# Inner rows of the first FFN and gated rows of the retention laid out in lanes, x moved by one spacer

## The chip, the cores and the metric

The kernel runs on one core of one Trainium2 chip. The metric is the device time of one execution in microseconds; lower is better. "TensorE", "VectorE" (DVE), "ScalarE" (ACT), "GpSimd" (POOL) and "SyncE" (SP) are the engines of the core. TensorE shows up in the profile twice: PE for the matmuls and PEld for the loads of their weights.

## The reference

One step of a two-layer streaming encoder on 288 frames (256 of a prompt, 32 of a running stream), width 2048, in fp32:

```python
# layer 0: gMLP mixer, then FFN; layer 1: retention mixer, then FFN
h, v = gmlp_mix(x, w_a_in, a_ln_g, a_ln_b, a_ws, a_bs, w_a_out)     # or
h, s = retention_mix(x, pos, states, w_b_in, w_b_out)
x = layer_norm(ALPHA * x + h, ln_mix_g[i], ln_mix_b[i])
x = layer_norm(ALPHA * x + swiglu(x, w_ffn_in[i], w_ffn_out[i]), ln_ffn_g[i], ln_ffn_b[i])

def swiglu(x, w_in, w_out):                  # hidden width 5632
    gate, up = jnp.split(x @ w_in, 2, axis=-1)
    return (jax.nn.silu(gate) * up) @ w_out
# end of retention_mix: o is normalised per head (8 heads of 512)
y = (jax.nn.silu(g) * o) @ w_out
```

The large products are `x @ w_in` and `(...) @ w_out` of the gMLP, of the retention and of the two FFNs. The inner rows are `silu(gate) * up`; the gated rows are `silu(g) * o`.

## The kernel before

**Products.** Every fp32 operand of a large product is split into two fp32r parts, high and low, with `hi = f` rounded and `lo = f - hi` (function `split`, a ScalarE copy at L655 and a VectorE subtraction at L656). A product of a 128x128 weight block with a 128x288 tile of rows is three matmuls that add into one PSUM tile: weight high with rows high (L123), weight high with rows low (L124), weight low with rows high (L125). The rows are the moving operand of 288 columns, one for each frame; each matmul has its own weight load.

**Weights.** They lie in HBM in the order of use, eight blocks to a chunk of 512 KB. `Core.prep` loads a chunk over the SP queue (tile `raw`), and splits it into `whi` and `wlo`. `Core.blk` hands out the next block and keeps three chunks ahead.

**Stages.** In order: `a_in` and `a_out` (gMLP), `f_in0` and `f_out0` (FFN of layer 0, in two halves of the hidden width: `f_in0` half 0, `f_out0` half 0, `f_in0` half 1, `f_out0` half 1), `b_in` and `b_out` (retention, in two groups of four heads: `b_in`, `b_out`, `b_in`, `b_out`), and `f_in1` and `f_out1`, again in two halves. In the profile, PSUM tiles carry these names with an `a` ahead (`af_out` is `f_out0` and `f_out1`, `ab_out` is `b_out`). TensorE's program is written out by hand and keeps its order. Each stage makes 16 or more output tiles of 128 rows, one after the other, over all k-tiles. The first four output tiles of a stage's `f_out` or `b_out` run interleaved with a lag of two k-tiles (`Core.group`), the other twelve one by one (`Core.tiles`). After a LayerNorm the first ten output tiles of the next `in` stage are made from rows that are not yet normalised, with eight more columns (`PostNorm.start`, 296 columns).

**Two layouts of rows.** Rows that come out of a stage and go into an `out` stage lie in plain tiles of 320 words for each k-tile (`moving`), behind four words (LEAD). `halves` reads them four words at a time: the last four of the first 144 columns, the last four of the second 144, then the four before, and so on down; PSUM is written in the same order. `x` lies in one tile of 10308 words, in lanes (`Lanes.view`): lane k has 36 blocks that lie 92 words apart (STEP), each with two cells of four words that lie 12 words apart (SIDE). The lanes of the 16 k-tiles, high and low, are interleaved with each other; where each begins is in the table PLACES, in units of four words.

**Two orders of products.** `Core.step` makes the three matmuls of one k-tile (L123 to L125). `Core.turn` takes four k-tiles at once and makes their twelve matmuls in the order of the table TURN (L134); PLACES and TURN belong together: each matmul begins 4 units before the one ahead of it, modulo 16 units. `Core.tiles` uses `turn` only where the rows are `x` (L196), and `step` for everything else and in the groups of four.

**Around it.** `Head` (retention) reuses the eight rooms of gated rows (tags `oh0` to `oh3` and `ol0` to `ol3`, 1280 words each) for the head's other data before the gated rows of that head are written (`pair`, `blocks`, `o_gate`). `rope` makes the rotary products on VectorE with two scratch tiles. The last stage keeps weights in the space of `x`, from word 60 on (L844). Spacers ("shift...") set where the tiles of each pool begin.

Of the kernel before, what the change touches and what calls it, by code (L numbers as in the profile page):

```python
# [10 lines left out]
F32 = mybir.dt.float32  # L11
# [41 lines left out]
TURN = ((0, 0), (1, 1), (1, 0), (0, 1), (2, 0), (0, 3), (0, 2), (1, 3), (1, 2), (2, 3), (2, 2), (2, 1))  # L53
GAMMA = [1.0 - 2.0 ** (-5 - h) for h in range(HEADS)]


class Core:
# [55 lines left out]
    def step(self, ps, w, k, m, x, first, last):  # L113
        mm = self.nc.tensor.matmul
        hi, lo = self.blk(w, k, m)
        xh, xl = x
        if len(xh.shape) == 4:
            n = 8 * xh.shape[1]
            wide, most = cells(ps[:, :n]), cells(ps[:, n - NT:n])
        else:  # L120
            wide = most = halves(ps)
            xh, xl = halves(xh), halves(xl)
        mm(wide, hi, xh, start=first, stop=False)  # L123
        mm(most, hi, xl, start=False, stop=False)  # L124
        mm(wide, lo, xh, start=False, stop=last)  # L125
        if self.soon:
            self.soon.pop()()

    def turn(self, ps, w, ks, m, x, first, last):
        b = [self.blk(w, k, m) for k in ks]  # L130
        v = [x(k) for k in ks]
        out = cells(ps[:, :NT])
        for i, (kind, j) in enumerate(TURN):
            self.nc.tensor.matmul(out, b[j][kind == 2], v[j][kind == 1], start=first and i == 0, stop=last and i == len(TURN) - 1)  # L134
        if self.soon:
            self.soon.pop()()
# [27 lines left out]
    def group(self, w, koff, ks, ms, x, evac, hook=None, lag=2):  # L164

        nk = len(ks)
        lag = [lag * j for j in range(len(ms))]
        ps = {}
        n = 0
        for s in range(nk + lag[-1]):  # L170
            done = []
            for j, m in enumerate(ms):
                i = s - lag[j]
                if 0 <= i < nk:
                    if i == 0:
                        ps[m] = (self.accum if j < 4 else self.bank)(f"a{w}_{m}_{self.ticks}")
                    self.step(ps[m], w, koff + ks[i], m, x(ks[i]), i == 0, i == nk - 1)
                    n += 1
                    if i == nk - 1:
                        done.append(m)  # L180
                    if n % nk == 0:
                        self.tick()
            if hook is not None:
                hook(s)
            for m in done:
                evac(m, ps[m])

    def tiles(self, w, koff, ks, ms, x, evac, grouped=True, lag=2):

        nk = len(ks)  # L190
        if grouped:
            self.group(w, koff, ks, ms[:4], x, evac, lag=lag)
            ms = ms[4:]
        for m in ms:
            p = self.accum(f"a{w}_{m}_{self.ticks}")
            if x == self.x:  # L196
                for i in range(0, nk, 4):
                    self.turn(p, w, ks[i:i + 4], m, x, i == 0, i == nk - 4)
            else:
                for i, k in enumerate(ks):  # L200
                    self.step(p, w, koff + k, m, x(k), i == 0, i == nk - 1)
            evac(m, p)
            self.tick()


class Lanes:


    def __init__(self, t):
        self.t = t  # L210

    def view(self, low, k, lead=0):
        t = self.t
        dims = [list(t.ap[0]), [STEP, NT // 8 + lead], [SIDE, 2], [1, 4]]
        return bass.AP(tensor=t.tensor, offset=t.offset + 4 * PLACES[low][k] - STEP * lead, ap=dims)

    def front(self, k, i):
        t = self.t
        dims = [list(t.ap[0]), [SIDE, 2], [1, 2]]
        return bass.AP(tensor=t.tensor, offset=t.offset + 4 * PLACES[0][k] - STEP + i, ap=dims)  # L220
# [4 lines left out]
    def led(self, k):  # L225
        return self.view(0, k, 1), self.view(1, k)
# [40 lines left out]
class PostNorm:  # L267
# [359 lines left out]
    def start(self, w, ms, evac):  # L627

        core, nc = self.core, self.nc
        x = self.x.led  # L630
# [38 lines left out]
def gmlp(core, cst, x, y, lnp, ins, v_out, begin, load):  # L669
    tc, nc = core.tc, core.nc  # L670
    xs = core.x
    with ExitStack() as es:
# [126 lines left out]
        core.tiles("a_out", 0, list(range(KT)), list(range(KT)), lambda k: (sh[:, k, :NT], late["sl"][:, k, :NT]),  # L799
# [4 lines left out]
def ffn(core, cst, x, y, lnp, layer, prev, out=None, rows=None):  # L804
    tc, nc = core.tc, core.nc
    xs = core.x
    ln = PostNorm(core, cst, x, y, lnp, 2 * layer + 1, out)
    with tc.tile_pool(name=f"ffn{layer}", bufs=1, reuse_waits="tile") as pool:
        if out is None:
            hh = moving(pool, HH, f"hh{layer}")  # L810
            hl = moving(pool, HH, f"hl{layer}")
        else:
            ln.tables(pool, rows)
            pool.tile([P, 36], F32, name="shift_hid")
            hid = pool.tile([P, HH, 2 * ROW], F32R, name="hid")[:, :, LEAD:]
            hh, hl = hid, moving(pool, HH, "hl1")
        for half in range(2):
            sg = {}

            def evac(m, ps):  # L820
# [4 lines left out]
                else:  # L825
# [4 lines left out]
                    split(nc, hh[:, i, :NT], hl[:, i, :NT], f)  # L830
# [17 lines left out]
            core.tiles(f"f_out{layer}", half * HH, list(range(HH)), list(range(KT - ends)),  # L848
                       lambda k: (hh[:, k, :NT], hl[:, k, :NT]),
                       ln.last if half else ln.part)  # L850
# [5 lines left out]
def retention(core, cst, x, y, lnp, prev, ins, st_p_out, st_s_out):  # L856
    tc, nc = core.tc, core.nc
    xs = core.x
    mm = nc.tensor.matmul
    wide = lambda out, l, r, **kw: mm(turned(out, 4), l, turned(r, 4), **kw)  # L860
    with ExitStack() as es:
        pool = es.enter_context(tc.tile_pool(name="ret", bufs=1, reuse_waits="tile"))
        oh, ol = {}, {}
        for i in range(8):
            pool.tile([P, 4 * ROW], F32, tag=f"o{'hl'[i % 2]}{i // 2}", name=f"r_room{i}")
# [15 lines left out]
        def pair(name, h):  # L881
            t = pool.tile([P, 4 * ROW], F32, tag=f"oh{h % 4}", name=name)
            return t[:, :2 * DV].rearrange("p (t f) -> p t f", t=2)

        def blocks(name, h):
            t = pool.tile([P, 4 * ROW], F32, tag=f"ol{h % 4}", name=name)
            return t[:, :4 * NT].rearrange("p (b i s) -> p b i s", b=9, i=4)

        def rope(dst, a, b, cos, sin, nm):
            t1 = pool.tile([P, NT], F32, tag="rt1", name=f"rt1{nm}", bufs=1)  # L890
            t2 = pool.tile([P, NT], F32, tag="rt2", name=f"rt2{nm}", bufs=1)
            nc.vector.tensor_tensor(t1, a[:, :NT], cos, ALU.mult)
            nc.vector.tensor_tensor(t2, b[:, :NT], sin, ALU.mult)
            nc.vector.tensor_tensor(dst[:, 0, :NT], t1, t2, ALU.subtract)
            nc.vector.tensor_tensor(t1, a[:, :NT], sin, ALU.mult)
            nc.vector.tensor_tensor(t2, b[:, :NT], cos, ALU.mult)
            nc.vector.tensor_tensor(dst[:, 1, :NT], t1, t2, ALU.add)

        class Head:
# [206 lines left out]
            def o_gate(self, what):  # L1106
# [6 lines left out]
                oh[h % 4] = moving(pool, 4, f"r_oh{h}", f"oh{h % 4}")  # L1113
                ol[h % 4] = moving(pool, 4, f"r_ol{h}", f"ol{h % 4}")
                for i in range(4):
                    split(nc, oh[h % 4][:, i, :NT], ol[h % 4][:, i, :NT], self.sg[:, i, :])
# [27 lines left out]
        for grp in range(2):  # L1144
            a, b, c, d = order[4 * grp:4 * grp + 4]
            ms = sum(a + b, []) + c[0] + d[0] + c[1] + d[1]
            if grp == 0:
# [4 lines left out]
                       lambda k: (oh[k // 4][:, k % 4, :NT], ol[k // 4][:, k % 4, :NT]),  # L1152
                       ln.last if grp else ln.part)
# [4 lines left out]
def hybrid_step(ctx, tc, ins, outs):  # L1158
# [5 lines left out]
    cp.tile([P, 4], F32, name="shift")  # L1164
    lnp.tile([P, 32], F32, name="shift_lnp")
    x = Lanes(cp.tile([P, LANES], F32R, name="x"))
    core.x = x.pair
# [119 lines left out]
```

## Time and profile before

| | |
|---|---|
| median of 3 runs | 2765.64 us (2765.02 to 2766.17) |
| the profiled execution | 2765.76 us, of which 2763.9 us from the first to the last instruction |
| TensorE busy | 2758.4 us, 100% of the span, 21614 matmuls |
| VectorE, ScalarE, GpSimd busy | 1717.5 us (62%), 1262.7 us (46%), 144.6 us (5%) |
| mean granted TensorE clock | 0.999 |
| data moved | 515.55 MB, 187 GB/s |

Matmuls are pipelined: one takes about 287 ns from its start to its end, but the next starts about 125 ns after it. What a matmul costs is therefore the distance from start to start, which is read from a stretch of time and the number of matmuls in it: the pieces of the chain of waits have a start, a length and a number; the table of stretches (windows) has the number of matmuls that touch each stretch, which is two more than the number that start in it.

### The profile page before, as it was taken

Reading aid. Unit: us, or ns where it says so; the run is one execution under the profiler, and the core shown is the slowest. Engines: PE = TensorE matmul, PEld = TensorE weight load, DVE = VectorE, ACT = ScalarE, POOL = GpSimd, SP = SyncE. Lnnn points to the kernel's source line nnn. Section 1 sums busy time; section 2 is a strip of 40 time slices with the busy share of each in tenths; the row PEclk is TensorE's granted clock in tenths of the full one; section 3 lists DMA queues with packets and bytes.
Section 4 is the critical chain, followed back from the end, with each engine's and each line's share of the span. In section 5 each row is a group of like instructions: output and inputs, shape, how many; then the busy total and the mean of one; then the engine's idle time right before and its main releaser. Section 6 shows DMA issues by size and latency. Waiting matters only on the chain.

```text
span 2763.9 us, 51981 instructions
## 1 busy us (share of the span) xinstructions
PE 2758.4 (100%) x21614; PEld 2748.0 (99%) x21614; DVE 1717.5 (62%) x2779; ACT 1262.7 (46%) x1747; POOL 144.6 (5%) x245
## 2 busy tenths in 40 slices
PE   9999999999999999999999999999999999999999
PEld 9999999999999999999999999999999999999999
DVE  6688964444444466877865666767854455444466
ACT  5454554433344444644543444545644433444444
POOL 1100000000000000012200121200000000000001
PEclk9999999999999999999999999999999999999999
DMA  8654555555555555567765666765455555555554
GB/s 281 217 191 160 171 177 176 177 170 171 175 175 175 181 169 178 171 218 239 243 195 169 201 218 220 230 200 170 169 176 175 177 172 175 171 173 169 173 170 142
DMA packets 147374, 515.55 MB, mean 187 GB/s; under 512 B 18161, under 2 KB 21377, under 8 KB 147105
## 3 DMA queue, kind: packets, MB, share of 16 engines
q1 hardware_dynamic: 132848, 473.62, 52.0%
q0 software_dynamic: 14288, 38.60, 4.5%
q8 instruction: 169, 2.77, 0.4%
q14 instruction: 69, 0.56, 0.1%
HBM read 486.99 MB, written 25.17 MB: 185 GB/s over the span
## 4 chain that ended last, share of the span: by engine, by line
PE 99%; DVE 1%; DMA 0%; issue 0%; POOL 0%; ACT 0%; POOLq 0%; DVEq 0%; ACTq 0%
PE af_in L134 34%; PE ab_in L134 19%; PE af_out L123 6%; PE af_out L124 6%; PE af_out L125 6%; PE aa_in L134 4%; PE ab_out L123 2%; PE ab_out L124 2%; PE ab_out L125 2%; PE af_in L123 2%; PE af_in L125 2%; PE af_in L124 1%; PE aa_out L123 1%; PE aa_out L124 1%; PE aa_out L125 1%; PE sp L860 1%
## 5 line engine op out<-in xcount | busy, mean ns | idle before, releaser
L656 DVE TENSOR_TENSOR wlo<-raw,whi 128x1024 fp32r<-128x1024 f32 (+1 forms) x884 | 1074.7, 1217 | 805.1 <-ACT whi L655 801.9
L655 ACT CAST whi<-raw 128x1024 fp32r<-128x1024 f32 (+1 forms) x884 | 924.7, 1046 | 1301.5 <-PE af_in L134 319.9
L134 PE MATMUL af_in<-x,whi 128*128 128x288 f32 x4992 | 808.5, 287 | 0.0
L134 PEld LDWEIGHTS af_in<-x,whi 128*128 128x128 f32 x4992 | 705.5, 187 | 0.0
L134 PE MATMUL af_in<-x,wlo 128*128 128x288 f32 x2496 | 516.0, 287 | 0.0
L134 PE MATMUL ab_in<-x,whi 128*128 128x288 f32 x2752 | 443.9, 287 | 0.0
L134 PEld LDWEIGHTS af_in<-x,wlo 128*128 128x128 f32 x2496 | 391.0, 187 | 0.0
L134 PEld LDWEIGHTS ab_in<-x,whi 128*128 128x128 f32 x2752 | 388.3, 187 | 1.3
L124 PE MATMUL af_out<-hl,whi 128*128 128x288 f32 x1320 | 383.2, 290 | 0.0
L134 PE MATMUL ab_in<-x,wlo 128*128 128x288 f32 x1376 | 283.2, 286 | 0.0
L124 PEld LDWEIGHTS af_out<-hl,whi 128*128 128x128 f32 x1320 | 247.8, 188 | 0.0
L134 PEld LDWEIGHTS ab_in<-x,wlo 128*128 128x128 f32 x1376 | 215.0, 187 | 0.0
L123 PE MATMUL af_out<-hh,whi 128*128 128x288 f32 x704 | 205.1, 291 | 0.0
L125 PE MATMUL af_out<-hh,wlo 128*128 128x288 f32 x704 | 202.9, 288 | 0.0
L123 PE MATMUL af_out<-hid,whi 128*128 128x288 f32 x616 | 178.4, 290 | 0.0
L125 PE MATMUL af_out<-hid,wlo 128*128 128x288 f32 x616 | 177.9, 289 | 0.0
L123 PE MATMUL ab_out<-r_oh,whi 128*128 128x288 f32 x512 | 149.0, 291 | 0.0
L124 PE MATMUL ab_out<-r_ol,whi 128*128 128x288 f32 x512 | 148.8, 291 | 0.0
L125 PE MATMUL ab_out<-r_oh,wlo 128*128 128x288 f32 x512 | 147.3, 288 | 0.0
L125 PEld LDWEIGHTS af_out<-hh,wlo 128*128 128x128 f32 x704 | 132.3, 188 | 0.2 <-DVE wlo L656 0.2
L123 PEld LDWEIGHTS af_out<-hh,whi 128*128 128x128 f32 x704 | 131.8, 187 | 0.0
L134 PE MATMUL aa_in<-x,whi 128*128 128x288 f32 x768 | 124.2, 287 | 0.0
(301 smaller groups left out, 3572.9 us busy)
## 6 DMA issues: line engine op xcount, KB each, us to landing
raw<-in_wpack_dram SPq DMA_DIRECT2D x883, 512.0 KB, 3.3
v_room<-tv POOLq DMA_DIRECT2D x32, 144.0 KB, 4.6
of<-o_room POOLq DMA_DIRECT2D x32, 144.0 KB, 5.6
vw<-v_room POOLq DMA_DIRECT2D x8, 512.0 KB, 6.0
out_st_s_dram<-sso POOLq DMA_DIRECT2D x16, 256.0 KB, 2.5
out_st_p_dram<-so POOLq DMA_DIRECT2D x16, 256.0 KB, 5.3
o_room<-to POOLq DMA_DIRECT2D x8, 512.0 KB, 3.8
g_room<-g_tv POOLq DMA_DIRECT2D x16, 144.0 KB, 4.3
```

The costliest lines, as they stand in the source:

```text
L123: mm(wide, hi, xh, start=first, stop=False)
L124: mm(most, hi, xl, start=False, stop=False)
L125: mm(wide, lo, xh, start=False, stop=last)
L134: self.nc.tensor.matmul(out, b[j][kind == 2], v[j][kind == 1], start=first and i == 0, stop=last and i == len(TURN) - 1)
L655: pin(nc.scalar.copy(hi, f))
L656: nc.vector.tensor_tensor(lo, f, hi.bitcast(F32), ALU.subtract)
L860: wide = lambda out, l, r, **kw: mm(turned(out, 4), l, turned(r, 4), **kw)
```

## The change

The inner rows of the first FFN (`f_out0`) are written into one tile `h` in lanes as x has them (92 and 12 words), with places of their own (INNER, 22 k-tiles). The gated rows of the retention (`b_out`) are written into the eight rooms, four lanes to a room, with 36 words from block to block and 12 or 76 words between the two cells (GATED); they are read from the last block to the first, and PSUM is written in the matching order, eight columns at a time from the end. The rooms grow from 1280 to 1344 words. Both are now multiplied by `turn`, four k-tiles at a time; where 22 k-tiles leave two over, the table TAIL has their six products. The groups of four output tiles still go through `step`, but read lanes. `f_out1` and `a_out` keep their plain tiles (class Plain, same reading order as before). `rope` writes its first product into its destination and needs one scratch tile instead of two. The spacer of four words in front of x goes; x and all tiles behind it begin 32 bytes earlier, against weights that stay where they are, and the weights kept in the space of x begin at word 64 instead of 60.

```diff
+TAIL = ((0, 0), (1, 1), (1, 0), (0, 1), (2, 0), (2, 1))
+INNER = ((18, 2566, 1722, 894, ...), (1674, 14, 1682, 2502, ...))
+WORDS = 13504
+GATED = ((8, 3), (12, 3), (0, 19), (4, 3))
+OROOM = 1344
...
-    def turn(self, ps, w, ks, m, x, first, last):
-        b = [self.blk(w, k, m) for k in ks]
-        v = [x(k) for k in ks]
-        out = cells(ps[:, :NT])
-        for i, (kind, j) in enumerate(TURN):
-            self.nc.tensor.matmul(out, b[j][kind == 2], v[j][kind == 1], start=first and i == 0, stop=last and i == len(TURN) - 1)
+    def turn(self, ps, w, koff, ks, m, x, first, last):
+        b = [self.blk(w, koff + k, m) for k in ks]
+        order = TURN if len(ks) == 4 else TAIL
+        for i, (kind, j) in enumerate(order):
+            low = int(kind == 1)
+            self.nc.tensor.matmul(x.out(ps, low), b[j][kind == 2], x.moving(low, ks[j]),
+                                  start=first and i == 0, stop=last and i == len(order) - 1)
...
-            if x == self.x:
+            if x.turns:
                 for i in range(0, nk, 4):
-                    self.turn(p, w, ks[i:i + 4], m, x, i == 0, i == nk - 4)
+                    self.turn(p, w, koff, ks[i:i + 4], m, x, i == 0, i + 4 >= nk)
...
+class Gated:
+    turns = True
...
+    def at(self, low, k):
+        first, side = GATED[(k + 2 * low) % 4]
+        return self.rooms[low][k // 4 % 4], 4 * first, 4 * side
...
+    def moving(self, low, k):
+        t, o, side = self.at(low, k)
+        n = NT // 8
+        return bass.AP(tensor=t.tensor, offset=t.offset + o + 36 * (n - 1), ap=[list(t.ap[0]), [-36, n], [side, 2], [1, 4]])
...
+    def out(self, ps, low):
+        return bass.AP(tensor=ps.tensor, offset=ps.offset + NT - 8, ap=[list(ps.ap[0]), [-8, NT // 8], [4, 2], [1, 4]])
...
-            hh = moving(pool, HH, f"hh{layer}")
-            hl = moving(pool, HH, f"hl{layer}")
+            h = Lanes(pool.tile([P, WORDS], F32R, name=f"h{layer}"), INNER)
...
-                    split(nc, hh[:, i, :NT], hl[:, i, :NT], f)
+                    split(nc, *h.pair(i), f if out is not None else cells(f))
...
-                    o = 60 + i * CB * P
+                    o = 64 + i * CB * P
...
-            t1 = pool.tile([P, NT], F32, tag="rt1", name=f"rt1{nm}", bufs=1)
-            t2 = pool.tile([P, NT], F32, tag="rt2", name=f"rt2{nm}", bufs=1)
...
+            t = pool.tile([P, NT], F32, tag="rt", name=f"rt{nm}", bufs=1)
+            for d, (u, v, op) in enumerate(((cos, sin, ALU.subtract), (sin, cos, ALU.add))):
+                r = dst[:, d, :NT]
+                nc.vector.tensor_tensor(r, a[:, :NT], u, ALU.mult)
+                nc.vector.tensor_tensor(t, b[:, :NT], v, ALU.mult)
+                nc.vector.tensor_tensor(r, r, t, op)
...
-                    split(nc, oh[h % 4][:, i, :NT], ol[h % 4][:, i, :NT], self.sg[:, i, :])
+                    split(nc, *gated.pair(4 * (h % 4) + i), cells(self.sg[:, i, :]))
...
-    cp.tile([P, 4], F32, name="shift")
```

On TensorE, the fifth output tile of `f_out0`, the first after the group of four, begins as follows before (tile names are output, rows, weights; `128x36x2x4` is the order of writing of `halves`):

```order
L123 MATMUL af_out_4_96_7065<-hh_3740,whi_6960 128x36x2x4
L124 MATMUL af_out_4_96_7065<-hl_3741,whi_6960 128x36x2x4
L125 MATMUL af_out_4_96_7065<-hh_3740,wlo_6961 128x36x2x4
L123 MATMUL af_out_4_96_7065<-hh_3740,whi_6960 128x36x2x4
L124 MATMUL af_out_4_96_7065<-hl_3741,whi_6960 128x36x2x4
L125 MATMUL af_out_4_96_7065<-hh_3740,wlo_6961 128x36x2x4
```

The same place with the change (L132 is the matmul in `turn`):

```order
L132 MATMUL af_out_4_96_7063<-h_3739,whi_6958 128x288 x4
L132 MATMUL af_out_4_96_7063<-h_3739,wlo_6959 128x288
L132 MATMUL af_out_4_96_7063<-h_3739,whi_6958 128x288 x4
L132 MATMUL af_out_4_96_7063<-h_3739,wlo_6959 128x288 x3
L132 MATMUL af_out_4_96_7063<-h_3739,whi_6958 128x288 x4
```

The number of matmuls and the blocks of weights are the same; within four k-tiles the three kinds of product are mixed, and the output is written as one run of 288 columns. The same tile ends so, with a last full turn of twelve (the first four rows) and the two k-tiles that are left over:

```order
L132 MATMUL af_out_4_96_7063<-h_3739,whi_7022 128x288 x4
L132 MATMUL af_out_4_96_7063<-h_3739,wlo_7023 128x288
L132 MATMUL af_out_4_96_7063<-h_3739,whi_7022 128x288 x4
L132 MATMUL af_out_4_96_7063<-h_3739,wlo_7023 128x288 x3
L132 MATMUL af_out_4_96_7063<-h_3739,whi_7022 128x288 x4
L132 MATMUL af_out_4_96_7063<-h_3739,wlo_7023 128x288 x2
```

The last two rows are the six products of TAIL. In `b_out` the fifth output tile read like the first fence before, with `r_oh` and `r_ol` (the rooms with the high and the low gated rows) for `hh` and `hl`. With the change it begins so, on TensorE:

```order
L132 MATMUL ab_out_220_16688<-r_oh_14235,whi_16583 128x36x8
L132 MATMUL ab_out_220_16688<-r_ol_14236,whi_16583 128x36x8 x2
L132 MATMUL ab_out_220_16688<-r_oh_14235,whi_16583 128x36x8
L132 MATMUL ab_out_220_16688<-r_oh_14235,wlo_16584 128x36x8
L132 MATMUL ab_out_220_16688<-r_oh_14235,whi_16583 128x36x8 x2
L132 MATMUL ab_out_220_16688<-r_ol_14236,whi_16583 128x36x8 x2
L132 MATMUL ab_out_220_16688<-r_oh_14235,wlo_16584 128x36x8 x3
```

There the output is written as 36 runs of eight columns, where it was written in 72 runs of four.

More of the change, by code (lines that the diff above doesn't have):

```diff
@@ L111, in state, with step @@
         return self.ready[c]
-    def step(self, ps, w, k, m, x, first, last):
+    def step(self, ps, w, koff, k, m, x, first, last):
         mm = self.nc.tensor.matmul
[L115 to L125, printed above, removed]
+        b = self.blk(w, koff + k, m)
+        for i, (j, low) in enumerate(((0, 0), (0, 1), (1, 0))):
+            mm(x.out(ps, low), b[j], x.moving(low, k), start=first and i == 0, stop=last and i == 2)
         if self.soon:
             self.soon.pop()()
-    def turn(self, ps, w, ks, m, x, first, last):
-        b = [self.blk(w, k, m) for k in ks]
-        v = [x(k) for k in ks]
-        out = cells(ps[:, :NT])
-        for i, (kind, j) in enumerate(TURN):
-            self.nc.tensor.matmul(out, b[j][kind == 2], v[j][kind == 1], start=first and i == 0, stop=last and i == len(TURN) - 1)
+    def turn(self, ps, w, koff, ks, m, x, first, last):
[5 more added lines that the diff above has]
+                                  start=first and i == 0, stop=last and i == len(order) - 1)
         if self.soon:
@@ L219, in front, with __init__, out, pair @@
         dims = [list(t.ap[0]), [SIDE, 2], [1, 2]]
[L220 removed]
+        return bass.AP(tensor=t.tensor, offset=t.offset + 4 * self.places[0][k] - STEP + i, ap=dims)
     def pair(self, k):
         return self.view(0, k), self.view(1, k)
[L225 to L226 removed]
+    def out(self, ps, low):
+        return cells(ps[:, :NT])
+class Led:
+    turns = False
+    def __init__(self, lanes):
+        self.lanes = lanes
+    def moving(self, low, k):
+        return self.lanes.view(low, k, 1 - low)
+    def out(self, ps, low):
+        return cells(ps[:, 8 * low:8 + NT])
+class Plain:
+    turns = False
+    def __init__(self, hi, lo):
+        self.tiles = hi, lo
+    def pair(self, k):
+        return tuple(t[:, k, :NT] for t in self.tiles)
+    def moving(self, low, k):
+        return halves(self.tiles[low][:, k, :NT])
+    def out(self, ps, low):
+        return halves(ps)
+class Gated:
+    turns = True
+    def __init__(self, hi, lo):
+        self.rooms = hi, lo
+    def at(self, low, k):
+        first, side = GATED[(k + 2 * low) % 4]
+        return self.rooms[low][k // 4 % 4], 4 * first, 4 * side
+    def view(self, low, k):
+        t, o, side = self.at(low, k)
+        return bass.AP(tensor=t.tensor, offset=t.offset + o, ap=[list(t.ap[0]), [36, NT // 8], [side, 2], [1, 4]])
+    def moving(self, low, k):
+        t, o, side = self.at(low, k)
+        n = NT // 8
+        return bass.AP(tensor=t.tensor, offset=t.offset + o + 36 * (n - 1), ap=[list(t.ap[0]), [-36, n], [side, 2], [1, 4]])
+    def pair(self, k):
+        return self.view(0, k), self.view(1, k)
+    def out(self, ps, low):
+        return bass.AP(tensor=ps.tensor, offset=ps.offset + NT - 8, ap=[list(ps.ap[0]), [-8, NT // 8], [4, 2], [1, 4]])
 def cells(v):
@@ L798, in gmlp @@
         ln = PostNorm(core, cst, x, y, lnp, 0)
-        core.tiles("a_out", 0, list(range(KT)), list(range(KT)), lambda k: (sh[:, k, :NT], late["sl"][:, k, :NT]),
+        core.tiles("a_out", 0, list(range(KT)), list(range(KT)), Plain(sh, late["sl"]),
                    lambda m, ps: ln.last(m, ps, True))
```

50 lines of the change are left out of this document (23 added, 27 removed).

## The prediction

> **What bounds the kernel now.** I read the page's engine shares and chain first, since they say which engine can pay anything back.
>
> ```profile
> PE 2758.4 (100%) x21614; PEld 2748.0 (99%) x21614; DVE 1717.5 (62%) x2779; ACT 1262.7 (46%) x1747; POOL 144.6 (5%) x245
> PEclk9999999999999999999999999999999999999999
> PE 99%; DVE 1%; DMA 0%; issue 0%; POOL 0%; ACT 0%; POOLq 0%; DVEq 0%; ACTq 0%
> L134 PE MATMUL af_in<-x,whi 128*128 128x288 f32 x4992 | 808.5, 287 | 0.0
> L124 PE MATMUL af_out<-hl,whi 128*128 128x288 f32 x1320 | 383.2, 290 | 0.0
> ```
>
> TensorE is the chain: 99% of it, at the full granted clock in all 40 slices, with no idle time before the large groups. Nothing is waited for there, so the time is the number of matmuls times their distance from start to start. The number stays at 21614; only the distance can change. A matmul's own length (287 and 290 ns above) hides it, because matmuls overlap. So I took stretches of one kind of matmul each, from the table of stretches for TensorE (from:to, length, PE busy, number of matmuls that touch the stretch, granted clock, DMA share, GB/s):
>
> ```profile
> 720.00:960.00 240.00, 240.00 (x1922) 1.00 0.53 176
> 575.00:705.00 130.00, 130.00 (x1011) 1.00 0.52 171
> 975.00:1015.00 40.00, 40.00 (x313) 1.00 0.53 178
> 1040.00:1100.00 60.00, 60.00 (x476) 1.00 0.55 180
> 1432.00:1525.00 93.00, 93.00 (x724) 1.00 0.51 171
> 1880.00:1940.00 60.00, 60.00 (x476) 1.00 0.52 173
> 2215.00:2340.00 125.00, 125.00 (x989) 1.00 0.52 173
> 2350.00:2600.00 250.00, 250.00 (x1950) 1.00 0.52 171
> ```
>
> Two matmuls in each count only reach into the stretch, so I divide by the count less two. The turned matmuls on x (first row, f_in0's second half): 240/1920 = 125.0 ns. f_out0's first half, plain rows and step: 130/1009 = 128.8. Its second half: 40/311 = 128.6 at first, 60/474 = 126.6 later. b_out's first group: 93/722 = 128.8; late in its second group 60/474 = 126.6. f_out1, also plain rows: 125/987 = 126.6. And the last row is the odd one: f_in1's second half has the same lanes of x, the same order and the same weights' places as the first row, and runs at 250/1948 = 128.3. The chain of waits gives the same prices over whole runs of turned matmuls (start, length, number):
>
> ```profile
> 368.52 204.05 PE af_in L134 x1632
> 708.68 264.00 PE af_in L134 x2112
> 1429.90 0.13 PE ab_out L123
> 1528.89 31.12 PE ab_in L134 x249
> 2009.11 204.05 PE af_in L134 x1632
> 2346.92 271.04 PE af_in L134 x2112
> ```
>
> 264.00/2112 = 125.00 against 271.04/2112 = 128.33; b_out's first group is (1528.89 - 1429.90)/768 = 128.89. The two halves of f_in0 and f_in1 that precede an f_out are both at 204.05/1632 = 125.03. So plain rows know two rates here, 128.89 and 126.67 (I take that for 126.6), and lanes know 125.0 and 128.33. Each holds for whole stages and turns over at a stage's start or after a stall, such as the one for the centering product in f_out0:
>
> ```profile
> 1015.22 0.14 PE cen L363
> ```
>
> **The change part by part.** (1) Turned tiles. 12 of 16 output tiles: f_out0 has 12 x 22 k-tiles x 3 products x 2 halves = 1584 matmuls, b_out 12 x 16 x 3 x 2 groups = 1152. What they cost now: f_out0's first half, 792 at 128.89. Its second half begins at the change from f_in0 (708.68 + 264.00 = 972.68); the group of four takes 264 x 0.12889 = 34.0 us, to 1006.7; until the centering at 1015.22 there are 66 more at 128.89, and the remaining 726 run at 126.67. b_out's first group has 576 at 128.89. In its second, the group of four and one more tile (48) are at 128.89 if the stall falls where it does in f_out0, one tile after the group's end; the other 528 are at 126.67. Together 1482 at 128.89 and 1254 at 126.67. The price with the change is bounded by the two rates of x in lanes, 125.0 and 128.33. I take 125.0: of 12768 turned matmuls in this trace (rows under rival C) 10656 are at 125.0 and 2112 at 128.33, and the new stages come straight after an x stage at 125.0. Gain 1482 x 3.89 + 1254 x 1.67 = 5.76 + 2.09 = 7.9 us; at 128.33 it would be 0.8 - 2.1 = -1.3.
>
> (2) The groups of four keep step but read lanes: 528 + 384 = 912 matmuls, now at 128.89. Step over lanes is in the trace twice:
>
> ```profile
> 30.00:53.00 23.00, 23.00 (x183) 1.00 0.86 285
> 315.00:365.00 50.00, 50.00 (x386) 1.00 0.51 169
> 1229.83 2.66 PE sp L860 x12
> ```
>
> a_in's first tiles: 23/181 = 127.1. f_in0's first ten tiles: 50/384 = 130.2, but two of three have 296 columns. A 512-column matmul on the same page costs 2.66/12 = 222 ns, so a column costs (222 - 125)/224 = 0.43 ns and the eight columns 3.5; two thirds of that off gives 127.9. I take 127.6: 912 x 1.3 = 1.2 us, between -1.2 (at 130.2) and 1.6.
>
> (3) TAIL: six products end with one jump that breaks the even steps. 24 tiles have it. By (2) such jumps cost 2 to 3 ns on average, so 0.1 us; 1 us if each upset several turns.
>
> (4) ScalarE and VectorE write lanes instead of plain rows: 76 splits. Lanes are priced in the trace by x's own split:
>
> ```profile
> L655 ACT CAST x<-y 128x288 fp32r<-128x288 f32 x64 | 26.8, 429 | 13.1 <-PE af_in L125 5.7 <-DMA y<-in_xT_dram 4.8 <-PE ab_in L125 2.5
> L655 ACT CAST hh<-hf 128x288 fp32r<-128x288 f32 x44 | 18.9, 430 | 2.6 <-DVE hf L829 2.6
> L656 DVE TENSOR_TENSOR x<-y,x 128x288 fp32r<-128x288 f32 x64 | 27.1, 451 | 6.2 <-ACT x L655 6.1
> L656 DVE TENSOR_TENSOR hl<-hf,hh 128x288 fp32r<-128x288 f32 x44 | 19.9, 451 | 0.6 <-ACT hh L655 0.5
> ```
>
> 429 against 430 ns and 451 against 451: nothing. rope keeps six VectorE operations per call, all in VectorE's own order, and VectorE is at 62%; nothing. What covers these is TensorE's 24 matmuls per weight chunk, 3.0 us at 125.0, against one ScalarE half of a weight split and one VectorE half:
>
> ```profile
> L656 DVE TENSOR_TENSOR wlo<-raw,whi 128x1024 fp32r<-128x1024 f32 (+1 forms) x884 | 1074.7, 1217 | 805.1 <-ACT whi L655 801.9
> L655 ACT CAST whi<-raw 128x1024 fp32r<-128x1024 f32 (+1 forms) x884 | 924.7, 1046 | 1301.5 <-PE af_in L134 319.9
> ```
>
> 1.05 and 1.22 us in each 3.0 leave over half of both engines free. With that cover gone, the 76 splits would cost at most 76 x 0.45 = 34 us on either engine. The first matmuls of f_out0 and b_out wait for the same weights as before, with no new wait on the rows.
>
> (5) x and all later tiles move 32 bytes against the weights. The trace has no other place for x. Its price is bounded by the same 125.0 and 128.33 on one side and, where it is now 128.33, by 125.0 on the other. Plain rows give the nearest hint: f_out0's and f_out1's lie in pools with different bases, and both show the same two rates. So I take the place to leave the rates alone: 0, between -35 and +7 us (rivals below).
>
> Sum: 7.9 + 1.2 - 0.1 = 9.0 us. The profiled execution took 2765.76 us, its span 2763.9 and 1.9 around it; 2756.8 is left. The median shown is 2765.64, 0.1 lower, inside the rounding: **2756.8 us**.
>
> **The rivals.** A: moving x also frees f_in1's second half. It is the one lane stage at 128.33, and it enters from f_out1's plain rows, which move too. 2112 x 3.33 = 7.0 us more: 2749.8. For it: the rate is a matter of where a stage locks in. Against: x, f_out1's rows and their distance to each other move together. 17%.
>
> B: the lanes are not what makes 125.0, and the new stages lock in at 128.33. For it: f_in1's second half is exactly that. Against: all other x stages, among them those right behind b_in's small products. Then (1) gives -1.3, and with (2) and (3) the sum is -0.2: 2765.9, no change. 13%. The Trainium skill, "TensorE: Matmul & The Clock Gate", Part 2, gives TensorE two independent SBUF read ports, so that loading weights takes nothing from the moving rows. By it the place of rows would not matter and the sum would be zero; the rows at 125.0, 126.6 and 128.8 for equal shapes disagree.
>
> C: slower. With x 32 bytes lower against the weights, its turned matmuls lock in at 128.33 in the stages that are at 125.0 now: f_in0 3744, b_in 4128, f_in1's first half 1632 and a_in 1152, together 10656:
>
> ```profile
> L134 PE MATMUL af_in<-x,wlo 128*128 128x288 f32 x2496 | 516.0, 287 | 0.0
> L134 PE MATMUL ab_in<-x,whi 128*128 128x288 f32 x2752 | 443.9, 287 | 0.0
> L134 PE MATMUL ab_in<-x,wlo 128*128 128x288 f32 x1376 | 283.2, 286 | 0.0
> L134 PE MATMUL aa_in<-x,whi 128*128 128x288 f32 x768 | 124.2, 287 | 0.0
> L134 PE MATMUL aa_in<-x,wlo 128*128 128x288 f32 x384 | 79.2, 287 | 0.1
> ```
>
> With the 4992 quoted first these are 12768, less the 2112 of f_in1's second half. All of them cost 35.5 us: 2765.7 - 9.0 + 35.5 = 2792. It decides from 4360 matmuls on, (9.0 + 5.5)/0.00333, two half stages and a bit. For it: the same addresses have been at 128.33 once. Against: behind b_in's small products the rate comes back to 125.0 each time, as in the two rows below (6.01/48 and 42.02/336). 12%.
>
> ```profile
> 1223.82 6.01 PE ab_in L134 x48
> 1232.49 42.02 PE ab_in L134 x336
> ```
>
> D: b_out is written to PSUM in runs of eight columns, backwards. Runs of four have never been under 126.6 here, one run of 288 is at 125.0. If runs cost, b_out's 1152 turned matmuls stay at 126.67: 1.9 us less gain, 2758.7. 8%. "PSUM — Partial Sum Buffer", Specifications, in the Trainium skill says that any non-contiguous pattern slows matmuls significantly; the trace bears out at most 1.6 ns in 125.
>
> **How the numbers follow.** Forecast 50%, A 17%, B 13%, C 12%, D 8%. 0.2% is 5.5 us, about what a measurement of this kernel can tell from no change. The forecast, A and D are faster by more than that (75%, of which I leave 2 to their weaker forms, with some stage turning over the wrong way): faster 0.73. B and the mild forms of C, one half stage lost (2763.9), are the same: 0.14. C proper is slower: 0.13. The range runs from A with the better end of (2), 2748, to the sum with two half stages of x lost, 2756.8 + 2 x 7.0 = 2771; I cut it at 2769, since one half stage or B lie well inside. Outside are C proper and A's extremes.
>
> **What would show it.** Right: the stretches of f_out0 and b_out after the group of four at 125.0 (1000 ns hold 8.0 starts), groups at 127 to 128, x stages unchanged. Step (1) falls if af_out or ab_out on the turn's line shows 126.7 or 128.3; (5) falls if a run of turned x matmuls in the chain leaves 125.0, or if f_in1's second half does; (4) if TensorE shows idle time before f_in's or f_out0's groups with a VectorE or ScalarE releaser. A new stage that turns over in the middle would make the sum wrong without making its mechanism wrong.

## The result and the profile after

| | before | after |
|---|---|---|
| median | 2765.33 us of 4 runs (2764.95 to 2766.17) | 2748.72 us of 4 runs (2748.63 to 2750.32) |
| ratio to before | | 0.9941, 95% interval 0.9924 to 0.9958 |
| the profiled execution's span | 2763.9 us | 2746.9 us |

The kernel became faster by 16.6 us, about twice the 9.0 that the sum gave. The page of the changed kernel, its engine shares, its clock and the share of the chain by engine:

```profile
PE 2741.2 (100%) x21614; PEld 2731.1 (99%) x21614; DVE 1714.8 (62%) x2779; ACT 1261.9 (46%) x1747; POOL 144.5 (5%) x245
PEclk9999999999999999999999999999999999999999
PE 99%; DMA 0%; DVE 0%; SPq 0%; ACT 0%; issue 0%; DVEq 0%; ACTq 0%
```

As many matmuls as before, at the same clock, and TensorE is still the whole chain. VectorE and ScalarE are as busy as they were. So nothing but the distance from start to start has changed. The chain of waits of the changed kernel gives it by stage (start, length, number):

```profile
571.03 33.47 PE af_out L123 x264
604.50 99.30 PE af_out L132 x792
703.80 264.02 PE af_in L132 x2112
967.82 33.47 PE af_out L123 x264
1001.29 8.29 PE af_out L132 x66
1009.71 91.07 PE af_out L132 x726
...
1422.44 24.59 PE ab_out L123 x192
1447.03 73.32 PE ab_out L132 x576
1520.35 60.00 PE ab_in L132 x480
...
1870.09 67.22 PE ab_out L132 x528
2000.05 204.01 PE af_in L132 x1632
2204.06 133.76 PE af_out L123 x1056
2337.82 264.00 PE af_in L132 x2112
```

The turned tiles of f_out0 come at 99.30/792 = 125.4 ns, near the 125.0 that was forecast. Those of b_out do not: 73.32/576 = 127.3, a rate that no turned tiles of before have. And the last row is f_in1's second half: 264.00 us where it was 271.04, so 125.0 ns instead of 128.33, on rows whose layout and order the change leaves as they were.

Since each stage begins where the one before it ends, the starts in this view give each stage's length. The difference to before, in us:

| stage | forecast | after | lanes and orders alone | spacer alone |
|---|---|---|---|---|
| f_out0, first half | -3.4 | -3.34 | -2.40 | -2.35 |
| f_out0, second half | -1.8 | -1.90 | -1.12 | -0.74 |
| b_out, first group | -2.5 | -1.07 | -0.37 | -1.71 |
| b_out, second group | -1.3 | +0.09 | +0.80 | -0.54 |
| f_in1, second half | 0 | -7.04 | 0 | -7.04 |
| f_out1, second half | 0 | -0.93 | 0 | -0.93 |
| all else of the span | 0 | -2.8 | -0.4 | -1.8 |
| span | -9.0 | -17.0 | -3.5 | -15.1 |

The forecast column is the prediction's terms laid out by stage: f_out0's first half, for instance, is 792 x 3.89 + 264 x 1.3 ns = 3.4 us. The last two columns are the first two experiments. "All else" holds a_in, whose length differs from run to run (200.7 to 202.3 us over all runs here); the -0.4 of the third column is a_in alone.

### The profile page after: what moved, and what is told of

Its sections match the earlier page's. It is cut to its first block, busy times and chain, and to the rows that moved or that the text cites. A ratio compares the mean times of both kernels' runs of the same rounds, so it can differ in the third digit from the quotient of the medians.

```text
span 2746.9 us, 51972 instructions
## 1 busy us (share of the span) xinstructions
PE 2741.2 (100%) x21614; PEld 2731.1 (99%) x21614; DVE 1714.8 (62%) x2779; ACT 1261.9 (46%) x1747; POOL 144.5 (5%) x245
## 4 chain that ended last, share of the span: by engine, by line
PE 99%; DMA 0%; DVE 0%; SPq 0%; ACT 0%; issue 0%; DVEq 0%; ACTq 0%
PE af_in L132 34%; PE ab_in L132 19%; PE af_out L123 11%; PE af_out L132 7%; PE ab_out L132 5%; PE aa_in L132 5%; PE af_in L123 5%; PE aa_out L123 4%; PE ab_in L123 2%; PE ab_out L123 2%; PE aa_in L123 2%; PE sp L923 1%; PE ob L923 1%; PE b L574 0%; PE p L566 0%; PE q L565 0%
## 5 line engine op out<-in xcount | busy, mean ns | idle before, releaser
L132 PE MATMUL af_in<-x,whi 128*128 128x288 f32 x4992 | 803.5, 286 | 0.0
L132 PEld LDWEIGHTS af_in<-x,whi 128*128 128x128 f32 x4992 | 701.4, 187 | 0.0
L132 PE MATMUL af_in<-x,wlo 128*128 128x288 f32 x2496 | 513.3, 286 | 0.0
L132 PE MATMUL ab_in<-x,whi 128*128 128x288 f32 x2752 | 443.7, 287 | 0.0
L132 PEld LDWEIGHTS af_in<-x,wlo 128*128 128x128 f32 x2496 | 389.4, 187 | 0.0
L132 PEld LDWEIGHTS ab_in<-x,whi 128*128 128x128 f32 x2752 | 387.8, 187 | 1.1
L132 PE MATMUL ab_in<-x,wlo 128*128 128x288 f32 x1376 | 283.0, 286 | 0.0
L132 PEld LDWEIGHTS ab_in<-x,wlo 128*128 128x128 f32 x1376 | 214.7, 187 | 0.0
L123 PE MATMUL af_out<-hl,whi 128*128 128x288 f32 x616 | 177.9, 289 | 0.0
L132 PE MATMUL af_out<-h,whi 128*128 128x288 f32 x1056 | 170.9, 287 | 0.0
L132 PEld LDWEIGHTS af_out<-h,whi 128*128 128x128 f32 x1056 | 148.8, 187 | 0.0
L123 PE MATMUL af_in<-x,whi 128*128 128x296 f32 (+1 forms) x640 | 124.6, 291 | 0.0
L132 PE MATMUL aa_in<-x,whi 128*128 128x288 f32 x768 | 124.3, 287 | 0.0
L123 PEld LDWEIGHTS af_out<-hid,wlo 128*128 128x128 f32 x616 | 115.6, 188 | 0.0
L123 PEld LDWEIGHTS af_out<-hl,whi 128*128 128x128 f32 x616 | 115.6, 188 | 0.0
L123 PEld LDWEIGHTS af_out<-hid,whi 128*128 128x128 f32 x616 | 115.6, 188 | 0.0
L132 PE MATMUL af_out<-h,wlo 128*128 128x288 f32 x528 | 108.8, 287 | 0.0
L132 PEld LDWEIGHTS aa_in<-x,whi 128*128 128x128 f32 x768 | 107.9, 187 | 0.0
```

What stands on the lines that cost most here:

```text
L123: mm(x.out(ps, low), b[j], x.moving(low, k), start=first and i == 0, stop=last and i == 2)
L132: self.nc.tensor.matmul(x.out(ps, low), b[j][kind == 2], x.moving(low, ks[j]), start=first and i == 0, stop=last and i == len(order) - 1)
```

## The experiments

Below, a row's or lane's **place** is where its reading begins (for gated rows that is the last block), counted in units of 16 bytes from the start of the weights' tiles, by the program's addresses. The lanes of one tile all have the same place modulo 4. x is at 2 modulo 4 before and at 0 modulo 4 after; the inner rows' lanes are at 0 modulo 4 and the gated rows' at 1 modulo 4 in the changed kernel, and at 2 and 3 where the spacer is put back into it.

### The two halves of the change, one at a time

The changed kernel with the spacer put back; x and all tiles behind it then lie as in the kernel before:

```diff
-                    o = 64 + i * CB * P
+                    o = 60 + i * CB * P
...
+    cp.tile([P, 4], F32, name="shift")
```

> The changed kernel with the four-word spacer in front of x again (and the kept weights from word 60): all tiles from x on lie 32 bytes higher against the weights, the lanes and the turned order stay. Theory P (the place of the rows against the weights picks which of its rates a stage takes): f_in1's second half goes back from 264.0 to about 271.0 us, f_out1's last stage back to about 141.6, a_out to about 98.9; f_out0 keeps 132.8 and 133.0. Time about 2748.7 + 7.0 + 0.9 + 0.5 + up to 2 for smaller stages = 2757 to 2759. Rival L (the lanes upstream free f_in1's second half by the state in which they leave TensorE): f_in1's second half stays at 264.0, time 2749 to 2751.

Measured: 2762.15 us (10 runs; before 2765.75 on the same chip), ratio 0.9987, interval 0.9978 to 0.9997. That is slower than the 2757 to 2759 that was expected. Its chain of waits, at f_out0's first half, at b_out's first group, and at the end:

```profile
572.15 33.79 PE af_out L123 x264
605.93 99.92 PE af_out L132 x792
...
1425.94 24.70 PE ab_out L123 x192
1450.64 73.92 PE ab_out L132 x576
...
2209.67 133.76 PE af_out L123 x1056
2343.43 271.04 PE af_in L132 x2112
```

With the spacer the turned tiles of f_out0 come at 126.2 ns and those of b_out at 73.92/576 = 128.33, and f_in1's second half is back at 271.04. f_out0's halves were expected to keep 132.8 and 133.0 us and took 133.7 each, so this part of the expectation was wrong. Lanes and orders without the move bring 3.5 us.

The 126.2 is a mean of the two prices that x has. The sixth, seventh and eighth tile of f_out0's first half, one tile of 66 matmuls each and one matmul of the tile ahead:

```profile
613.94 8.38 PE af_out L132 x67
622.20 8.59 PE af_out L132 x67
630.66 8.39 PE af_out L132 x67
```

The seventh is at 8.59/67 = 128.2 ns, its neighbours at 125.1 and 125.2, and so it goes on to the end of the half: every third tile is slow. Each tile ends in the jump of TAIL; x and b_out, whose order has no jump, hold one rate. That the jump turns the rate over is thus likely, but it was not tried at this place.

The other half: the kernel before without its spacer, and nothing else changed.

```diff
-                    o = 60 + i * CB * P
+                    o = 64 + i * CB * P
...
-    cp.tile([P, 4], F32, name="shift")
```

> The kernel before without the spacer and nothing else of the change: all rows 32 bytes lower against the weights, plain rows and step as before. Theory P: f_in1's second half 264.0 us (-7.0), f_out1's last stage 140.7 (-0.9), a_out 98.4 (-0.5), f_in stages -0.3 each; and if plain rows then take 126.67 ns everywhere, f_out0 about 133.8 and 134.0 (-2.3, -0.9) and b_out 97.3 and 97.4 (-1.7, -0.5): 2765.3 - 15 = about 2750. If plain rows keep 128.89 in f_out0 and b_out: 2755 to 2756. Rival L: f_in1's second half stays at 271.0, time 2764 to 2766.

Measured: 2751.01 us (2749.77 to 2751.39, 4 runs), ratio 0.9945, interval 0.9931 to 0.996. The move alone brings 14.7 of the 16.6 us. In its table of stretches (from:to, length, PE busy, matmuls that touch the stretch, clock, DMA share, GB/s) stand f_out0's first half, b_out's first group, and f_in1's second half:

```profile
575.00:700.00 125.00, 125.00 (x989) 1.00 0.53 173
1430.00:1515.00 85.00, 85.00 (x674) 1.00 0.53 174
2345.00:2595.00 250.00, 250.00 (x2002) 1.00 0.53 176
```

Less two for each count: plain rows and step are at 125/987 = 126.6 and 85/672 = 126.5 where the kernel before had 128.8 and 128.8, and x is at 250/2000 = 125.0. So the move took away the plain rows' slow rate and x's slow rate at once, with the old layout and the old order of products. On top of it the lanes and turns bring f_out0 another 1.0 and 1.2 us, and cost b_out 0.6 us in each group (table above, the column after less the column of the spacer alone).

### The place against the weights, or the rows' own place

Without the spacer the rows move and the weights stay. To tell the two apart, the rows were left where they are in the kernel before, and the weights moved 32 bytes the other way:

```diff
-        self.wp.tile([P, 16], F32, tag="shift", name="shift_wp", bufs=1)
+        self.wp.tile([P, 24], F32, tag="shift", name="shift_wp", bufs=1)
...
-                    o = 60 + i * CB * P
+                    o = 64 + i * CB * P
...
-    cp.tile([P, 4], F32, name="shift")
```

(The weights' spacer stands ahead of the weights and of all rows, and grows by 32 bytes; x's spacer, which with its padding takes 32 bytes, goes. So the weights lie 32 bytes further on and the rows where they were.)

> The kernel before, rows at exactly their addresses of before, but the weights' buffers begin 32 bytes higher (their spacer grows from 16 to 24 words, the spacer in front of x goes, and the kept weights follow to word 64). Theory P (the place of the rows against the weights): every stage as in the run with only the spacer gone: f_in1's second half 264.0 us, f_out0 133.8 and 134.1, b_out 97.3 and 97.4; time 2750 to 2752. Rival Q (the rows' own address decides, or the space at the end of memory): stages as before, f_in1's second half 271.0, f_out0 136.1, time 2764 to 2767.

Measured: 2749.33 us (one run; before 2765.56). The stretches of f_out0's first half and of f_in1's second half:

```profile
575.00:700.00 125.00, 125.00 (x990) 1.00 0.53 173
2345.00:2595.00 250.00, 250.00 (x2002) 1.00 0.53 177
```

Again 126.5 and 125.0, and all stages but a_in agree with the run with the spacer alone within 0.1 us. Rows at their old addresses have the new rates, so it is not their own address that sets the rate; the two runs share the distance between rows and weights. (Rows and weights moved together, at an unchanged distance, were not run.) The Trainium skill, "TensorE: Matmul & The Clock Gate", Part 2, describes two independent SBUF read ports, by which loading weights takes nothing from the moving rows. This run doesn't fit that: 32 bytes of the weights' address alone are worth 7.04 us in one stage of 2112 matmuls.

The weights' tiles are not only loaded by TensorE, they are also written by the splits on ScalarE and VectorE. The trace of before speaks against these writes as the cause: in f_in1's second half every six matmuls take 770 ns (128.33 each), while the two engines are idle as while they are busy. What in the chip ties rows and weights together no run here shows.

### What comes ahead of a stage

At the old place x had both rates: 125.0 in f_in0 and f_in1's first half, 128.33 in f_in1's second. The stage ahead of the slow one is f_out1. In the kernel before, only f_out1's rows were moved, by 32 bytes:

```diff
-            pool.tile([P, 36], F32, name="shift_hid")
+            pool.tile([P, 44], F32, name="shift_hid")
```

> The kernel before, with only f_out1's rows 32 bytes higher (their own spacer grows from 36 to 44 words), so that they lie against x and the weights as f_out0's rows do; x, weights and all else stay. Theory E (which of its two rates x takes is set by the stage it comes from): f_in1's second half runs as f_in0's, 264.0 us instead of 271.0; f_out1 as f_out0: first part 136.1 instead of 133.8, and its last part stays within 1 us. Time 2765.7 - 7.0 + 2.3 = about 2761. Rival X (x's own place against the weights sets it): f_in1's second half stays at 271.0; time 2765 to 2768.

Measured: 2760.91 us (one run; before 2765.56). A stretch of f_out1's first half, and one of f_in1's second:

```profile
2215.00:2345.00 130.00, 130.00 (x1011) 1.00 0.52 171
2355.00:2605.00 250.00, 250.00 (x2002) 1.00 0.53 176
```

f_out1 went to 130/1009 = 128.8 and its first half lost 2.35 us, and x behind it, which nobody moved, came to 125.0 and gained 7.0. f_in1's second half also writes its inner rows into the tiles that were moved. That is not what slows it: in the kernel before, the first such write starts at 2359.8 us, and x was at its slow rate ahead of that. Its first matmuls in the chain of before, and for comparison those of f_in0's second half:

```profile
2346.92 12.83 PE af_in L134 x100
708.68 12.88 PE af_in L134 x103
```

They come at 128.3 and 125.0 ns. So at its old place x has two rates, and the stage ahead decides which. In the kernel before and in this run x is at 125.0 behind plain rows at 128.9, and at 128.33 behind plain rows at 126.7; whether the rate of these rows or their place decides is open.

Does x at its new place depend on that too? The same edit was made in the changed kernel (with the rooms of the gated rows moved as further below):

> The kernel with the rooms 16 bytes on, and f_out1's rows 32 bytes higher than there, so that x comes from rows at another place against it and the weights. Theory S (at its new place x has the one rate of 125.0, whatever it comes from): f_in1's second half stays at 264.0 us, f_out1 stays at 133.8 or goes to 136.1; time 2746 to 2749. Rival E2 (the stage it comes from still decides): f_in1's second half goes to 271.0, time 2753.

Measured: 2747.08 us (one run; before 2764.45). In the chain, f_out1's first half and f_in1's second:

```profile
2201.84 133.76 PE af_out L123 x1056
2335.60 264.00 PE af_in L132 x2112
```

f_out1's rows now lie against the weights as in the kernel before, and take the same 133.76 us, but x behind them stays at 125.0. Wherever it lay at 0 modulo 4 it was at 125.0, after whatever stage; that it has no slow rate there at all is not shown.

### What cost b_out its gain

Rival D held that the runs of eight in which b_out writes PSUM would cost. Here b_out writes one run of 288 columns, and f_out0 writes 36 runs of eight in its place. What is left out is the order: the columns of these two products come out permuted over the frames.

```diff
-        return bass.AP(tensor=ps.tensor, offset=ps.offset + NT - 8, ap=[list(ps.ap[0]), [-8, NT // 8], [4, 2], [1, 4]])
+        return cells(ps[:, :NT])
...
-            h = Lanes(pool.tile([P, WORDS], F32R, name=f"h{layer}"), INNER)
+            h = Inner(pool.tile([P, WORDS], F32R, name=f"h{layer}"), INNER)
```

`Inner` is `Lanes` with the method `out` that the first line takes away.

> The changed kernel, but b_out's matmuls write PSUM in one run of 288 columns, and f_out0's write it in 36 runs of eight from the end (as b_out's did). The columns of both products then lie in another order in PSUM, so their results are permuted over the frames; number, size and reading of the matmuls are unchanged. Theory W (the order of writing costs): b_out's turned matmuls go from 127.3 to 125.0 ns, its stages from 97.9 and 98.05 us to about 96.3; f_out0's turned matmuls go from 125.35 to about 127.3, its stages from 132.8 and 133.0 to about 134.4. Theory R (the rooms' place or stride costs, not the writing): all four stages stay within 0.2 us.

Measured: 2749.05 us (one run; before 2765.75). The chain at f_out0's first half and b_out's first group:

```profile
571.38 33.47 PE af_out L123 x264
604.85 99.30 PE af_out L132 x792
...
1422.78 24.59 PE ab_out L123 x192
1447.38 73.32 PE ab_out L132 x576
```

All four lengths are those of the changed kernel to the hundredth. Between these two ways of writing PSUM there is no difference here; runs of four were not tried. "PSUM — Partial Sum Buffer", Specifications, in the Trainium skill says that a non-contiguous pattern slows matmuls significantly; for runs of eight fp32 columns against one run of 288 these rows show no difference.

The other suspect was where the rooms' lanes begin. They were put 16 bytes on, from 1 to 2 modulo 4:

```diff
-        return self.rooms[low][k // 4 % 4], 4 * first, 4 * side
+        return self.rooms[low][k // 4 % 4], 4 * first + 4, 4 * side
```

> The changed kernel with every lane of the gated rows begun 16 bytes later in its room, so that they begin at even units (2, 6, 10, 14 modulo 16) instead of odd ones (1, 5, 9, 13), as x (0, 4, 8, 12) and the inner rows (0, 4, 8, 12) do. Theory R (the odd place is what keeps b_out at 127.3 ns): the turned matmuls go to about 125.0, b_out's stages from 97.9 and 98.05 to about 96.3 us. Theory W, or the stride of 36 words read backwards as the cause: both stages stay within 0.3 us.

Measured: 2745.86 us (one run; before 2765.75). b_out's two groups in the chain:

```profile
1422.30 24.55 PE ab_out L123 x192
1446.86 72.01 PE ab_out L132 x576
...
1868.46 66.01 PE ab_out L132 x528
```

72.01/576 = 125.0 ns, from 127.3. The place did it: nothing else was changed. The two groups come to 96.56 and 96.70 us, 2.4 and 1.3 below before: what the prediction had for them (2.5 and 1.3). The same kernel was timed:

> The kernel with the rooms 16 bytes on, unchanged, timed in rounds: 2745 to 2747 us, 0.7% under the kernel before and about 0.1% under the changed kernel; the profile as in the single look (b_out 96.6 and 96.7 us).

Measured: 2746.09 us (2745.89 to 2746.64, 5 runs), ratio 0.9926, interval 0.9913 to 0.994 (before 2765.56). That is faster than the kernel before. It was not run side by side with the changed kernel, against which the chain shows 2.7 us less in b_out's two groups.

### Lanes without their order

With the rooms so placed, inner and gated rows kept their lanes but went through `step`:

```diff
-    turns = True
+    turns = False
...
+            h.turns = False
```

> The kernel with the rooms 16 bytes on, with lanes for inner and gated rows as there, but all their tiles made by step (high-high, low-high, high-low of one k-tile after the other) instead of turn. Theory O (the order is needed, since it makes each matmul begin 4 units before the last): the twelve tiles go to the rate of the groups of four: f_out0 from 132.8 and 133.0 to about 133.9 and 134.1, b_out from 96.6 and 96.7 to about 98.2: 2745.9 + 5.5 = about 2751. Rival Y (the layout alone is enough): the stages stay within 0.3 us, 2746.

Measured: 2752.67 us (one run; before 2765.56). f_out0's first half and b_out's first group are each one row of the chain now:

```profile
571.51 134.19 PE af_out L123 x1056
1425.88 98.15 PE ab_out L123 x768
```

127.1 and 127.8 ns. That is worse than plain rows with step at the new place (133.76 and 97.28 us in the run with the spacer alone). So the lanes by themselves bring nothing; the 125.0 needs the order of `turn`. That what counts in this order is the even step of 4 units is not shown by this run, which replaces the whole order; the next run bears on it.

### The products that are left over

TAIL ends with a jump. Its last two products were exchanged:

```diff
-TAIL = ((0, 0), (1, 1), (1, 0), (0, 1), (2, 0), (2, 1))
+TAIL = ((0, 0), (1, 1), (1, 0), (0, 1), (2, 1), (2, 0))
```

> The kernel with the rooms 16 bytes on, and the last two products of TAIL exchanged: where one jump of eight units off the even steps came at the end of each f_out0 tile, now come two of four. Theory: the 0.35 ns above 125.0 in f_out0's turned tiles (23 ns a tile, 24 tiles) are the jump; with two jumps they change, by at most 0.6 us either way. Rival: they are not the jump, f_out0 stays at 132.77 and 132.95 us within 0.03.

Measured: 2746.42 us (one run; before 2764.45), which by itself tells nothing from 2746.09. The chain does, since such lengths repeat to the hundredth:

```profile
605.19 99.08 PE af_out L132 x792
1001.74 8.29 PE af_out L132 x66
1010.16 90.92 PE af_out L132 x726
```

Against 99.30, 8.29 and 91.07: 0.37 us less in 24 tiles. At 125.0 ns the 1584 matmuls would take 198.00 us; they took 198.66 with the first TAIL and 198.29 with this one. By the starts of the tiles, a full tile of 66 takes 8.273 us with the first TAIL and 8.253 with this one, where 8.250 would be even steps: the one jump of eight units costs 23 ns, the two of four cost 3. The rest of the 0.66 us falls on the first turned tile of each half and on the centering.

### Does the place count modulo 4 alone?

If only the place modulo 4 counted, all rows could move by 64 bytes and nothing would change. The version with the moved rooms, with a spacer of 16 words ahead of x:

```diff
-                    o = 64 + i * CB * P
+                    o = 48 + i * CB * P
...
+    cp.tile([P, 16], F32, name="shift")
```

> The kernel with the rooms 16 bytes on, and a spacer of 16 words in front of x: all rows 64 bytes (4 units) higher against the weights, and the kept weights from word 48, so that they lie as the other weights do. The lanes begin at four places 4 units apart, so a shift by 4 units maps these places onto each other. Theory M (lanes repeat every 4 units): all lane stages as without the spacer: x at 125.0 ns, f_out0 132.8 and 133.0 us, b_out 96.6 and 96.7. Plain rows lie at one place, 4 for f_out1: by the run in which only f_out1's rows were moved its first part goes to 136.1 (+2.3) and its last part to 141.7 (+1). Time 2746 to 2750. Rival N (each 32 bytes matter on their own): some lane stage leaves 125.0, time above 2751.

Measured: 2754.02 us (one run; before 2764.45), where 2746 to 2750 was expected. The chain, at a_out after its centering, f_in0's second half, f_out0, b_out in both groups, f_in1's second half, and f_out1 after its centering:

```profile
238.64 69.81 PE aa_out L123 x528
608.70 99.26 PE af_out L132 x792
707.96 264.02 PE af_in L132 x2112
...
1451.35 73.92 PE ab_out L132 x576
...
1868.94 6.16 PE ab_out L132 x48
1875.24 66.00 PE ab_out L132 x528
...
2341.78 264.00 PE af_in L132 x2112
2647.72 59.55 PE af_out L123 x462
```

x and the inner rows kept their rates (125.0; 99.26 against 99.30). Plain rows did not: a_out is at 69.81/528 = 132.2 ns, the slowest that plain rows were in any run here, and f_out1's end at 59.55/462 = 128.9. f_out1's first half, which was expected to go to 136.1 us, stayed at 133.76. And the gated rows, at 2 modulo 4 as in the version that was timed, have 128.33 in the whole first group and, in the second, for the one tile ahead of the centering (6.16/48); after that stall they are at 125.0. So for x and the inner rows modulo 4 was enough in what was tried; plain rows depend on more than that, and for gated rows 2 modulo 4 is, like x's old place, one with two rates. Both groups start on the slow one here, and in the second the stall is where it ends. Why they start on it stays open.

## Why the prediction was right and wrong

It said faster, and it was; the time lies in the range, near its lower end, 8 us under the sum and 1.1 under rival A's 2749.8. But most of the gain came out of the step that was put at nothing. That the time is inside the range at all is luck: the lower end, 2748, is called A with the better end of (2), but A is 2749.8 and that end is worth 0.4 us more, which makes 2749.4, and 2748.72 is below it.

**What bounds the kernel.** Right: TensorE is 99% of the chain before and after, the count of matmuls stayed, and the gain is one of start to start. Rates hold over long stretches and repeat from run to run, but not always for whole stages: with the spacer back, f_out0 changes between its two rates from tile to tile.

**(1) Turned tiles, 7.9 us.** The price of 125.0 held in f_out0 (125.4) and failed in b_out (127.3), which lost 2.6 us of its term. The step took it that lanes in this order have the two prices of x and no third. Lanes at 1 modulo 4 have a third, and the run with the rooms 16 bytes on shows that the place is the cause. The hit in f_out0 is partly luck too: -3.34 and -1.90 match the forecast, but at x's old place the same lanes gave -2.40 and -1.12, and -2.35 and -0.74 are what the plain rows gain from the move alone. The step's reference, plain rows at 128.89, was itself gone at the new place.

**(2) Groups of four, 127.6 ns.** 33.47/264 = 126.8 in f_out0, 24.59/192 = 128.1 in b_out. Mean 127.3; the size was right. But at the new place plain rows would have been at 126.7, so laying these groups in lanes costs a little there.

**(3) TAIL, 0.1 us.** It was mis-sized: the jump costs 23 ns in each of 24 tiles, about 0.55 us, where 2 to 3 ns were taken. That lies below the bound of 1 us that was kept for it.

**(4) Splits and rope, 0.** Right: VectorE's busy time went from 1717.5 to 1714.8 us, ScalarE's from 1262.7 to 1261.9, and both hold 0% of the chain.

**(5) Moving x, 0.** This is the step that failed. Alone, the move made the kernel 14.7 us faster. The argument was that plain rows in pools with different bases show the same two rates, so that the place leaves rates alone. But it is the place that decides which of the two a stage gets: with the spacer gone, plain rows are at 126.6 in f_out0 and b_out, and with f_out1's rows at another place they go to 128.8. Its bounds, from 35 us of loss to 7 of gain, missed too: the gain end is f_in1's second half alone (7.04 measured), and the plain rows of f_out0 and b_out, which move with x, gained another 5.3 at the new place, f_out1's second half 0.9.

**The rivals.** A happened: f_in1's second half was freed, with the 7.0 us that A gave it. That A's time is hit within 1.1 us is partly luck: b_out fell 2.8 us short of the sum, and f_out1's second half and the remaining stages, which A left alone, made up for it. What was held against A, that x, f_out1's rows and their distance move together, left out the weights: the distance to them changes, and the run with the weights moved shows that this is enough. At x's old place it counts as well where f_out1's rows lie, as the run with only these moved shows. B was half right in a way that didn't matter: with the spacer back, b_out's lanes do lock at 128.33, and every third tile of f_out0 is there. C did not happen; x's new place is better than its old one, and the slow end was seen only at the old. D's loss happened in b_out, but not by its mechanism: runs of eight against one run in PSUM make no difference, and the lanes' place does.

## What to carry to other kernels

Where TensorE is the whole chain, divide the length of each stage by its matmuls: stages of equal shape at 125.0, 126.7, 128.3 and 128.9 ns point to where the operands lie. Before a layout is rewritten, the distance between the moving rows and the weights' tiles can be tried in steps of 16 and 32 bytes; here 32 bytes of distance were worth 14.7 us and the rewritten rows 2 more, or 5 once they were put at a better place themselves. A stage's rate can also hang on the stage ahead of it, so each such trial has to be read over all stages.

## What the hardware showed that was not expected

- The rate of matmuls with equal shapes took these values by the place of the rows against the weights: 125.0 (turned lanes at 0 and at 2 modulo 4), 128.33 (at 2 and at 3), 127.3 (at 1), 126.7, 128.9 and 132.2 (plain rows). Moving either operand by 32 bytes does the same.
- At some places there are two rates, and the one that a stage gets depends on what ran ahead of it: x at its old place is at 125.0 or 128.33 by where f_out1's rows lie. It then holds for 2112 matmuls without a change, whether ScalarE and VectorE are busy or not.
- Writing PSUM in 36 runs of eight columns or in one run of 288: 73.32 us for 576 matmuls in both.
- What ties the rows' place to the weights' addresses, what in the stage ahead picks the rate, whether x at 0 modulo 4 has a slow rate at all, and why the gated rows at 2 modulo 4 locked at 128.33 once, are open.
